# Two-layer DiT trunk with expert mixers: transposed adaptive-norm weights, and the gathered tile's choice of experts moved into the expert loop

## Chip, cores and metric

The kernel runs on one core of one Trainium2 chip. The metric is the device time of one execution in microseconds (us). The engines are named as in the profile: PE (TensorE), PEld (its weight loads), DVE (VectorE), ACT (ScalarE), POOL (GpSimd) and SP (SyncE, which issues most transfers).

## The reference

512 latent tokens of width 1024 go through two layers. Each layer has a mixer (layer 0: latent attention and neighbourhood attention over a shared input projection; layer 1: a conformer convolution) and then an expert mixer with 16,384 experts. Every sub-layer is normalised and modulated by parameters computed from the conditioning vector:

```python
sh1, sc1, g1, sh2, sc2, g2 = ada_params(c, w_ada[l], b_ada[l])     # split(silu(c) @ w + b, 6)
h_lat = h_lat + g1 * mixer(modulate(rms_norm(h_lat, g_norm1[l]), sh1, sc1))
h_lat = h_lat + g2 * peer_ffn(modulate(rms_norm(h_lat, g_norm2[l]), sh2, sc2), ...)

# peer_ffn, per token
q = (hb @ w_query).reshape(128, 8, 2, 128)                 # 8 heads, 2 halves
s = einsum("thpd,hpnd->thpn", q, sub_keys)                 # 16 score rows of 128
s_top, i_top = lax.top_k(s, 16)
best, pos = lax.top_k(s_top[:, :, 0, :, None] + s_top[:, :, 1, None, :], 16)   # of 256 pairs
expert = i_top[0] * 128 + i_top[1] at pos ; gate = softmax(best)
act = gelu(einsum("thkd,td->thk", u_tab[expert], hb))
y = einsum("thk,thkd->td", gate * act, v_tab[expert])
```

`w_ada[l]` is 1024 x 6144. A block below is 128 of its 6144 output features, so there are 48 blocks per layer: 0 to 7 shift 1, 8 to 15 scale 1, 16 to 23 gate 1, 24 to 31 shift 2, 32 to 39 scale 2, 40 to 47 gate 2.

## The kernel before

**Stages.** A preamble loads and normalises and computes blocks 0 to 15 of layer 0 with PE from rows of `w_ada` (L890). The projections follow (`quarter`-wise, each with a weight load, a split into high and low parts `w_hi` and `w_lo`, and three matmuls per product, L145 to L147), then the softmax units of the attention, the out-projection, the expert mixer of layer 0, the convolution, and the expert mixer of layer 1.

**The expert mixer (`peer`).** Of the four tiles of 128 tokens, three (384 tokens) are multiplied densely with all 128 chunks of 128 experts; the fourth, called the gathered tile here, fetches for each token its 128 experts' rows by indirect transfers and works on them with DVE.
- Front: 16 turns `hp`, one for each score row. Turn `hp` issues the load of query weights `wq[hp + 2]` on SP (`load_u`, tile `u_raw`, 3 buffers), 24 matmuls on PE, the split of `wq[hp + 1]` (ACT `u_hi`, POOL `u_lo` L176), the scores of `hp - 1` (L260, copied by ACT L263 to `sc`, 4 buffers), and on DVE `top16` of those scores (two maxima, a replacement and two index searches per tile, for the four tiles in turn) and after each second turn `stage2` (four additions and another `top16`). All queues are in program order and are never reordered.
- Seven dense chunks (EARLY) and beside them `ahead`: gates, ranks and expert numbers (`common`, `numbers`).
- 24 steps of `gbuild`: one-hot tables (L456, 128 x 4096) make the gates of all experts, which go to DRAM (`Gd`) and come back per chunk (`g_in`), while more dense chunks run until 32 are in the ring.
- Expert loop: 96 turns. In each, PE computes the activations of chunk m + 32 (`s1`) and the outputs of chunk m (`s2`, L605); SP loads `u_raw` and `v_raw` (512 KB each); ACT and DVE split them (`u_lo` L176, `v_lo` L584), and DVE makes the weighted activations `w` (L591) and `w_lo` (L596). The gathered tile starts with `decode_last` (9 steps of `lookup`, three a turn), and after it 236 of its 256 row steps lie in the remaining turns. A step is one indirect load on POOL (L616, five `row` buffers) and one DVE product (L624 for the first 128, L628 for the rest).
- Tail: 32 turns with `s2` alone and the last 20 row steps.

**Adaptive-norm blocks (`Ada`).** The other 80 blocks are computed beside other work, each from a load of 512 KB (`ada_w`, 128 x 8 x 128, input features on partitions):
- blocks 16 to 23 of layer 0 in the projections: 8 products on DVE (L766, L768) into `ada_acc`, and a matmul with ones (L907);
- blocks 24 to 39 in the softmax units: products and additions on POOL (L779 to L782), a transpose on PE (L900), and a sum and an addition on DVE (L902, L903);
- 14 blocks of layer 1 in the front of layer 0's mixer (`on_pe`): 8 matmuls each (L819 for columns, L821 for gate rows), 4 more in its `gbuild` steps (`side`), 8 in the front of layer 1's mixer;
- 30 blocks in the expert loop of layer 0 (`slow`): 8 products on DVE over three turns (L866, L868) and one matmul on PE (L883 or L886), which writes into the spare quarter of the `s1` bank.

The gate blocks (`g1`, `g2`) are wanted as rows that stand on all partitions. They go to DRAM as a 128 x 1024 table, block by block, and are loaded from there (`g1b`, `hg`).

## Time and profile before

| | us |
|---|---|
| median of three runs | 3344.88 |
| the profiled execution | 3343.83 |
| its span | 3342.1 |
| PE busy | 3207.8 (96%) |
| DVE busy | 2576.0 (77%) |
| ACT busy | 1288.2 (39%) |
| POOL busy | 976.1 (29%) |
| DMA moved | 764.34 MB, 229 GB/s |

One of the three runs was disturbed (5339.81 us); the other two are 3340.55 and 3344.88. The page divides the span into 40 equal slices and gives the busy share of each engine in tenths; its last lines are the granted clock of PE, the share of the 16 DMA engines and the GB/s:

```profile
PE   8889999988999999999999998988999999999999
```

Each digit is 83.6 us. PE is at nine tenths or more nearly everywhere; the eights are the first 250 us, 668 to 836 us, 2005 to 2089 us and 2172 to 2339 us (the second and the fourth are the one-hot tables of the two layers). Boundaries of the stages, read from the timeline of PE (us from the start of the span): projections 47 to 205, softmax units to 460, out-projection to 504, front of layer 0's mixer to 645, early chunks and ranks to 703, `gbuild` to 875, expert loop to 1671, tail to 1804, convolution to 2062, front of layer 1's mixer to 2187, one-hot tables from 2245, expert loop 2411 to 3204, tail to the end.

### The profile page before, as it was taken

How to read it: one execution, taken by the hardware profiler on the slowest of the kernel's cores; microseconds unless marked ns; L12 is line 12 of the kernel's file. 1: busy time of each engine (PE TensorE's matmuls, PEld its weight loads, DVE VectorE, ACT ScalarE, POOL GpSimd, SP SyncE). 2: the span in 40 equal slices, each digit the busy share in tenths (PEclk: the TensorE clock that was granted, in tenths of full speed). 3: DMA queues.
4: the chain of work that ended last, by engine and by line, in shares of the span. 5: the costliest groups of instructions: out<-in, count | busy, mean ns of one | idle time of the engine just before them, and what ended most of it. 6: DMA issues, size and time to landing. Idle time of an engine off the chain costs nothing.

```text
span 3342.1 us, 45728 instructions
## 1 busy us (share of the span) xinstructions
PE 3207.8 (96%) x16982; PEld 2783.6 (83%) x16982; DVE 2576.0 (77%) x4732; ACT 1288.2 (39%) x2065; POOL 976.1 (29%) x800
## 2 busy tenths in 40 slices
PE   8889999988999999999999998988999999999999
PEld 5775568978999999999987867888999999999987
DVE  3657736889688888888876976899777777777777
ACT  3435533345433333333335234235533333333333
POOL 1347412300033333443430001320033333344330
PEclk9989999999999999999999998999999999999999
DMA  6412124346799999899893113326789888989985
GB/s 199 130 46 79 57 82 152 114 164 252 269 337 328 324 342 333 318 339 336 307 320 119 51 45 112 117 86 247 266 285 314 313 310 315 313 309 314 314 311 180
DMA packets 373679, 764.34 MB, mean 229 GB/s; under 512 B 24144, under 2 KB 221008, under 8 KB 366160
## 3 DMA queue, kind: packets, MB, share of 16 engines
q1 hardware_dynamic: 292816, 442.62, 38.8%
q0 software_dynamic: 73728, 268.47, 22.9%
q10 hardware_dynamic: 6912, 50.33, 3.7%
q8 instruction: 133, 2.18, 0.3%
q14 instruction: 90, 0.74, 0.1%
HBM read 702.61 MB, written 58.72 MB: 228 GB/s over the span
## 4 chain that ended last, share of the span: by engine, by line
PE 83%; DVE 11%; issue 3%; DMA 1%; ACT 1%; SPq 1%; POOL 0%; ACTq 0%; POOLq 0%; DVEq 0%
PE acc L605 30%; PE s L145 11%; PE s L147 11%; PE s L146 11%; DVE eij L456 3%; PE y L1636 2%; PE cz L145 2%; PE cz L147 2%; PE cz L146 2%; DVE ahl L458 1%; PE z L147 1%; PE z L145 1%; PE z L146 1%; PE ot L1421 1%; DVE u_lo L176 1%
## 5 line engine op out<-in xcount | busy, mean ns | idle before, releaser
L146 PE MATMUL s<-hhi,u_lo 128*128 128x384 f32 (+1 forms) x2304 | 791.2, 343 | 14.4 <-DVE u_lo L176 14.2
L145 PE MATMUL s<-hhi,u_hi 128*128 128x384 f32 (+1 forms) x2304 | 798.6, 347 | 3.0 <-ACT u_hi L172 3.0
L147 PE MATMUL s<-hlo,u_hi 128*128 128x384 f32 (+1 forms) x2304 | 790.6, 343 | 0.0
L616 POOL DMA_INDIRECT row<-in_u_dram,eidx x256 | 313.2, 1224 | 954.2 <-DVE row L624 455.7
L616 POOL DMA_INDIRECT row<-in_v_dram,eidx x256 | 348.8, 1362 | 518.8 <-DVE gacc L628 448.4
L582 ACT ACTIVATE v_hi<-v_raw 128x1024 fp32r<-128x1024 f32 x192 | 203.8, 1062 | 679.0 <-PE acc L605 609.9
L146 PEld LDWEIGHTS s<-hhi,u_lo 128*128 128x128 f32 x2304 | 436.2, 189 | 33.2 <-DVE u_lo L176 17.4
L584 DVE TENSOR_TENSOR v_lo<-v_raw,v_hi 128x1024 fp32r<-128x1024 f32 x192 | 235.2, 1225 | 291.4 <-ACT v_hi L582 275.8
L145 PEld LDWEIGHTS s<-hhi,u_hi 128*128 128x128 f32 x2304 | 436.4, 189 | 18.8 <-ACT u_hi L172 3.7
L147 PEld LDWEIGHTS s<-hlo,u_hi 128*128 128x128 f32 x2304 | 435.6, 189 | 10.2
L605 PE MATMUL acc<-v_hi,w_hi 128*128 128x512 f32 x1344 | 417.4, 391 | 0.8 <-ACT w_hi L593 0.8
L605 PE MATMUL acc<-v_hi,w_lo 128*128 128x512 f32 x1344 | 416.2, 391 | 0.0
L605 PE MATMUL acc<-v_lo,w_hi 128*128 128x512 f32 x1344 | 415.9, 390 | 0.0
L176 DVE TENSOR_TENSOR u_lo<-u_raw,u_hi 128x1024 fp32r<-128x1024 f32 x242 | 295.1, 1219 | 48.1 <-ACT u_hi L172 48.0
L628 DVE SCALAR_TENSOR_TENSOR gacc<-row,gwgt,gacc 128x1024 f32<-128x1024 f32 x254 | 325.6, 1282 | 4.7
L172 ACT ACTIVATE u_hi<-u_raw 128x1024 fp32r<-128x1024 f32 x288 | 302.3, 1050 | 14.6 <-ACT stg L475 11.0
L624 DVE SCALAR_TENSOR_TENSOR row<-row,hg 128x1024 f32<-128x1024 f32 x256 | 300.6, 1219 | 0.0
L605 PEld LDWEIGHTS acc<-v_lo,w_hi 128*128 128x128 f32 x1344 | 252.3, 188 | 55.9
L605 PEld LDWEIGHTS acc<-v_hi,w_lo 128*128 128x128 f32 x1344 | 252.2, 188 | 54.6
L605 PEld LDWEIGHTS acc<-v_hi,w_hi 128*128 128x128 f32 x1344 | 249.5, 188 | 40.8 <-ACT w_hi L593 1.2
L593 ACT ACTIVATE w_hi<-w_f 128x384 fp32r<-128x384 f32 x256 | 134.7, 526 | 319.5 <-DVE w_f L591 315.8
L313 ACT ACTIVATE ring<-s 128x384 f32<-128x384 f32 x256 | 125.8, 491 | 318.8 <-PE s L147 318.8
(442 smaller groups left out, 4917.6 us busy)
## 6 DMA issues: line engine op xcount, KB each, us to landing
u_raw<-in_uT_dram SPq DMA_DIRECT2D x256, 512.0 KB
v_raw<-in_v_dram SPq DMA_DIRECT2D x192, 512.0 KB
Gd<-stg ACTq DMA_DIRECT2D x48, 1024.0 KB
g_in<-Gd SPq DMA_DIRECT2D x128, 384.0 KB
ada_w<-in_w_ada_dram SPq DMA_DIRECT2D x80, 512.0 KB
u_raw<-in_v_dram SPq DMA_DIRECT2D x64, 512.0 KB
u_raw<-in_wq_dram SPq DMA_DIRECT2D x32, 512.0 KB
ada_w<-in_w_ada_dram SPq DMA_DIRECT2D x8, 1024.0 KB
```

The lines of the kernel that those rows point to most:

```text
L145: nc.tensor.matmul(out, lhsT=lh, rhs=rh, start=first, stop=False)
L146: nc.tensor.matmul(out, lhsT=ll, rhs=rh, start=False, stop=False)
L147: nc.tensor.matmul(out, lhsT=lh, rhs=rl, start=False, stop=last)
L172: nc.scalar.activation(uh, u, AF.Copy)
L176: lo_eng.tensor_tensor(ul, u, uh.bitcast(F32), op=OP.subtract)
L582: nc.scalar.activation(vh, v, AF.Copy)
L584: nc.vector.tensor_tensor(vl, v, vh.bitcast(F32), op=OP.subtract)
L593: nc.scalar.activation(wh, w, AF.Copy)
L605: nc.tensor.matmul(acc[tt][hf], lhsT=w[:, s], rhs=v[:, hf * 512:(hf + 1) * 512], start=f and n == 0, stop=l and n == 2)
L616: nc.gpsimd.indirect_dma_start(out=r, out_offset=None, in_=un if n < 128 else vn, in_offset=bass.IndirectOffsetOnAxis(ap=eidx[:, c:c + 1], ...
L624: nc.vector.scalar_tensor_tensor(r, r, 1.0, hg, op0=OP.mult, op1=OP.mult, accum_out=act[:, c:c + 1])
L628: nc.vector.scalar_tensor_tensor(gacc, r, wgt[:, c:c + 1], gacc, op0=OP.mult, op1=OP.add)
```

## The change

**Adaptive-norm blocks.** `w_ada` is laid out transposed in DRAM (`wT_ada`, output features on partitions). A block is two halves; each is a load of 256 KB and one DVE `scalar_tensor_tensor` (128 x 512) against `crow`, the row silu(c) that stands on all partitions, with its sum over the free axis accumulated into one column. The tile has two buffers and one load is issued ahead. Neither PE nor POOL takes part, and after each eighth block come two small additions and, for gate blocks, a store to a DRAM row that `gate_row` later reads back on all partitions. `crow` is made in the preamble.

```diff
+    def blocks(self, pool, blocks, pause=0):
+        nc, todo, loaded = self.k.nc, [(f, i) for f in blocks for i in range(2)], []
+        def load():
+            if todo:
+                f, i = todo.pop(0)
+                t = pool.tile([128, D // 2], F32, name="ada_w", bufs=2)
+                nc.sync.dma_start(t, self.wT[f * 128:(f + 1) * 128, i * 512:(i + 1) * 512])
+                loaded.append((f, i, t))
+        load()
+        yield
+        while loaded:
+            load()
+            f, i, t = loaded.pop(0)
+            nc.vector.scalar_tensor_tensor(t, t, 1.0, self.k.crow[:, i * 512:(i + 1) * 512], op0=OP.mult, op1=OP.mult,
+                                           accum_out=self.half[:, f % 8:f % 8 + 1] if i else self.par[:, f:f + 1])
+            if f % 8 == 7 and i:
+                o = slice(f - 7, f + 1)
+                nc.vector.tensor_tensor(self.half, self.half, self.bT[:, o], op=OP.add)
+                nc.vector.tensor_tensor(self.par[:, o], self.par[:, o], self.half, op=OP.add)
+                if f // 8 in self.gate:
+                    nc.sync.dma_start(self.gate[f // 8].rearrange("f p -> p f"), self.par[:, o])
+            for _ in range(1 + pause):
+                yield
...
-    A2 = modulation(k, k.const, g2T[1], ada1.par, 32, "A2_1")      # was behind conv, now ahead of it
```

| where | blocks before | blocks after |
|---|---|---|
| projections | 8 (DVE and PE) | 24, three halves each quarter |
| softmax units | 16 (POOL, PE and DVE) | 20, two halves a call |
| front, layer 0 mixer | 14 (PE) | 16, three halves a turn in turns 0 to 10 |
| `gbuild`, layer 0 mixer | 4 (PE) | none |
| expert loop, layer 0 | 30 (DVE, one matmul) | 12, one half every third turn |
| front, layer 1 mixer | 8 (PE) | none |
| expert loop, layer 1 | none | 8, one half every fourth turn |

**The gathered tile.** In the front, `top16` and `stage2` run over the three dense tiles alone. The fourth tile's scores go to DRAM from ACT's queue, 64 KB a turn. `common` (gates and ranks) also runs over three tiles, and its three copies for the gathered tile fall away. In the expert loop `decode_last` loads the scores back (two loads of 512 KB) and does 16 `top16`, 8 `stage2`, the gates, ranks and lookups on DVE, paced by a table of estimated microseconds. Its gathers begin where the paced sum ends, in turn 15.

```diff
+        nc.scalar.dma_start(Sd[:, hp, :], sc[:, ND, :])
+        pend.append((hp, sc[:, 0:ND]))
...
-            for _ in range(DEC_MAIN):
-                if next(dec, dec) is dec:
+            while m and gfirst is None and spent < DEC_MAIN * m:
+                step = next(dec, None)
+                if step is None:
                     gfirst = m
                     for n in range(PF - LATE):
                         fetch(n)
-                    break
+                else:
+                    spent += step
             goal = 0
         elif m < busy:
-            goal = 236 * (m - gfirst) // (busy - 1 - gfirst)
+            goal = 226 * (m - gfirst) // (busy - 1 - gfirst)
         else:
-            goal = min(256, 236 + (m + 1 - busy))
+            goal = min(256, 226 + -(-30 * (m + 1 - busy) // 25))
```

`DEC_MAIN` is 4.2 now (estimated microseconds a turn), where it was 3 (steps a turn). The weighted activation `w` is computed in place in the ring's tile. All of this is done in both layers.

How the rows of DVE stand in the front of layer 0's mixer: `sc` are the scores of one turn, `S1v` their maxima, `cand` the pair sums, `gp` the PSUM tile of an adaptive-norm block, `crow` the row of silu(c). Before, the first two turns:

```order
L811 TENSOR_TENSOR ada_br<-gp,ada_br 128x128 x2
L222 MAX S1v<-sc 128x8 x4
L224 MATCH_REPLACE s_4295<-S1v,sc 128x128 x4
L226 MAX S1v<-s_4295 128x8 x4
L228 MAX_INDEX I_4061<-S1v,sc 128x8 x4
L230 MAX_INDEX I_4061<-S1v,s_4295 128x8 x4
L811 TENSOR_TENSOR ada_br<-gp,ada_br 128x128
```

After, the same place:

```order
L785 SCALAR_TENSOR_TENSOR ada_w,ada_half_84<-ada_w,crow 128x512
L785 SCALAR_TENSOR_TENSOR ada_w,ada_par_83<-ada_w,crow 128x512
L218 MAX S1v<-sc 128x8 x3
L220 MATCH_REPLACE s_4238<-S1v,sc 128x128 x3
L222 MAX S1v<-s_4238 128x8 x3
L224 MAX_INDEX I_4032<-S1v,sc 128x8 x3
L226 MAX_INDEX I_4032<-S1v,s_4238 128x8 x3
L785 SCALAR_TENSOR_TENSOR ada_w,ada_half_84<-ada_w,crow 128x512
L785 SCALAR_TENSOR_TENSOR ada_w,ada_par_83<-ada_w,crow 128x512
L785 SCALAR_TENSOR_TENSOR ada_w,ada_half_84<-ada_w,crow 128x512
```

Ahead of each turn's maxima DVE now has three products, each of which reads a load, and the maxima are three instead of four.

SP's queue at the same place, where `u_raw` is the load of query weights and `ada_w` that of a block or half block. Before:

```order
L167 DMA u_raw<-in_wq_dram 128x1024
L758 DMA ada_w<-in_w_ada_dram 128x8x128
L167 DMA u_raw<-in_wq_dram 128x1024
L758 DMA ada_w<-in_w_ada_dram 128x8x128
L167 DMA u_raw<-in_wq_dram 128x1024
```

After:

```order
L163 DMA u_raw<-in_wq_dram 128x1024
L778 DMA ada_w<-in_wT_ada_dram 128x512 x3
L163 DMA u_raw<-in_wq_dram 128x1024
L778 DMA ada_w<-in_wT_ada_dram 128x512 x3
L163 DMA u_raw<-in_wq_dram 128x1024
```

One load between two loads of query weights has become three of half the size, and each of them can be issued only when the product before last on DVE has freed its buffer.

PE's queue at the end of the second turn, where `scp` are the scores and `gp` the block. Before:

```order
L145 MATMUL s_4228<-hhi,u_hi 128x512
L146 MATMUL s_4228<-hhi,u_lo 128x512
L147 MATMUL s_4228<-hlo,u_hi 128x512
L821 MATMUL gp<-ada_w,cond 128x128 x16
L260 MATMUL scp<-skt,qt 128x128 x4
L145 MATMUL s_4318<-hhi,u_hi 128x512
```

After:

```order
L142 MATMUL s_4256<-hhi,u_hi 128x512
L143 MATMUL s_4256<-hhi,u_lo 128x512
L144 MATMUL s_4256<-hlo,u_hi 128x512
L256 MATMUL scp<-skt,qt 128x128 x4
L142 MATMUL s_4345<-hhi,u_hi 128x512
```

The matmuls of the blocks are gone from PE (two blocks in this turn, one in the others), and nothing takes their place.

## Rows read from the trace of the kernel before

**Rows 1.** Stretches: length, busy us of PE, PEld, DVE, ACT, POOL, clock, share, GB/s
```profile
504.00:660.00 156.00, 149.86 (x865) 133.18 (x864) 120.71 (x821) 50.23 (x76) 50.85 (x25) 0.98 0.41 135
875.00:1671.00 796.00, 795.24 (x4050) 724.30 (x4049) 682.73 (x1030) 288.81 (x383) 303.73 (x238) 1.00 0.92 327
2410.00:3205.00 795.00, 795.00 (x4020) 723.54 (x4019) 608.17 (x766) 291.80 (x387) 304.72 (x241) 1.00 0.89 308
1675.00:1700.00 25.00, 25.00 (x112) 20.72 (x111) 17.04 (x22) 8.91 (x12) 7.35 (x5) 1.00 1.00 370
```

**Rows 2.** Timeline of PE in the front: start us, us, engine, line, operation
```profile
535.43 0.48 PE L145 MATMUL s<-hhi,u_hi 128*128 128x512 f32 x1
...
540.99 1.95 PE L821 MATMUL gp<-ada_w,cond 128*128 128x128 f32 x16
542.77 1.06 PE L260 MATMUL scp<-skt,qt 128*128 128x128 f32 x8
543.59 0.48 PE L145 MATMUL s<-hhi,u_hi 128*128 128x512 f32 x1
```

**Rows 3.** Timeline of DVE in the front, idle time before it in brackets
```profile
544.50 0.88 DVE L222 MAX8 S1v<-sc 128x8 f32<-128x128 f32 x4 [3.19 <-ACT sc L263]
...
549.19 0.21 DVE L237 TENSOR_TENSOR cand<-S1v 128x64 f32<-128x64 f32 x1
...
553.20 0.27 DVE L811 TENSOR_TENSOR ada_br<-gp,ada_br 128x128 f32<-128x128 f32 x1
```

**Rows 4.** Groups of the whole span: line, shapes xcount, busy us, mean ns, idle before
```profile
L624 DVE SCALAR_TENSOR_TENSOR row<-row,hg 128x1024 f32<-128x1024 f32 x256 | 300.6, 1219 | 0.0
...
L596 DVE TENSOR_TENSOR w_lo<-w_f,w_hi 128x384 fp32r<-128x384 f32 x256 | 141.8, 554 | 44.3 <-ACT w_hi L593 44.3
...
L624 DVE DVE_READ_ACCUMULATOR row<-row,hg 128x1 f32 x256 | 21.1, 82 | 0.0
```

**Rows 5.** Line 768: count, nanoseconds min/median/max, first and last start
```profile
L768 DVE SCALAR_TENSOR_TENSOR ada_acc<-ada_w,cond,ada_acc x56: 350/352/2585, 80.1 to 204.4; 128x128 f32<-128x128 f32 x56
```

**Rows 6.** Chain of waits: a 64 KB and a 512 KB load; start us, us
```profile
164.81 2.23 DMA ada_br<-in_b_ada_dram
...
869.74 4.76 DMA ada_w<-in_w_ada_dram
```

**Rows 7.** Timeline of PE in the projections: where it sat idle
```profile
147.20 0.80 PE L147 MATMUL z<-w_lo,aTl 128*128 128x512 f32 x1 [4.83 <-DVE w_lo L1043]
...
169.21 0.79 PE L147 MATMUL z<-w_lo,aE 128*128 128x512 f32 x1 [5.97 <-DVE w_lo L1043]
...
204.81 0.49 PE L907 MATMUL tp<-ada_acc,ones 128*128 128x128 f32 x2 [3.90 <-DVE ada_acc L768]
```

**Rows 8.** Groups of DVE in the softmax units
```profile
L903 DVE TENSOR_TENSOR ada_par<-ada_par,vec 128x1 f32<-128x1 f32 x16 | 16.5, 1030 | 0.6
```

**Rows 9.** Groups of POOL in the front of layer 0's mixer
```profile
L176 POOL TENSOR_TENSOR u_lo<-u_raw,u_hi 128x1024 fp32r<-128x1024 f32 x21 | 51.1, 2434 | 102.9 <-ACT u_hi L172 102.8
```

**Rows 10.** Timeline of DVE: its wait at the first split behind each front
```profile
675.97 1.23 DVE L176 TENSOR_TENSOR u_lo<-u_raw,u_hi 128x1024 fp32r<-128x1024 f32 x1 [8.38 <-ACT u_hi L172]
...
2218.21 1.23 DVE L176 TENSOR_TENSOR u_lo<-u_raw,u_hi 128x1024 fp32r<-128x1024 f32 x1 [4.55 <-ACT u_hi L172]
```

**Rows 11.** Groups of DVE between that split and the one-hot tables
```profile
L367 DVE COPY d_ab<-stg 128x1024 f16<-128x1024 f16 x2 | 1.3, 686 | 0.0
```

**Rows 12.** Line 456, the one-hot tables: layer 0, then layer 1
```profile
L456 DVE TENSOR_TENSOR eij<-iota,ij x24: 2273/2284/2289, 703.2 to 838.8; 128x4096 f16<-128x4096 f16 x24
...
L456 DVE TENSOR_TENSOR eij<-iota,ij x24: 2283/2284/2295, 2245.5 to 2375.2; 128x4096 f16<-128x4096 f16 x24
```

**Rows 13.** Chain of waits: outputs of three turns of the expert loop
```profile
892.65 4.13 PE acc L605 x18
...
901.18 4.12 PE acc L605 x18
...
909.49 4.12 PE acc L605 x18
```

More of the change, by code (lines that the diff above doesn't have):

```diff
@@ L1 @@
 from contextlib import ExitStack
+from itertools import chain
 import numpy as np
@@ L263, in scores @@
         nc.scalar.activation(sc, p, AF.Copy)
-        pend.append((hp, sc))
+        nc.scalar.dma_start(Sd[:, hp, :], sc[:, ND, :])
+        pend.append((hp, sc[:, 0:ND]))
     ur, us = {}, {}
-    front_step = front and front(qp, lambda: psf.tile([128, TT, 128], F32, name="gp", bufs=4))
+    beside = front(qp) if front is not None else iter(())
     for hp in range(16):
@@ L280, in peer @@
             us[0] = split_u(ur.pop(0), nc.gpsimd)
-        if front_step is not None:
-            front_step()
-            if hp in FRONT_TWICE:
-                front_step()
+        for _ in range(3):
+            next(beside, None)
         qt = qp.tile([128, T], F32, name="qt", bufs=2)
@@ L314, in s1_gelu @@
         ring[c] = r
-    while front_step is not None and front_step():
-        pass
     for c in range(EARLY):
@@ L389, in peer @@
     tr = {}
-    rk = []
+    rk = gp.tile([128, ND, 2, 128, 2], F16, name="d_ab")
     def common():
-        gates_a()
-        yield from ranks(lambda n, shape, dt: gp.tile(list(shape), dt, name=n), TT * 128)
-        gates_b()
+        gates_a(gates, best)
+        room = gp.tile([128, 128, SB], F32, name="stg", bufs=2).rearrange("p a b -> p (a b)").bitcast(F16)
+        yield from ranks(pos.rearrange("p t h k -> p (t h k)"), room, rk)
+        gates_b(gates, gz)
         yield
-        for n, d_ in enumerate((a2l, b2l)):
-            nc.vector.tensor_copy(d_, rk[0][:, ND, n])
-        nc.vector.tensor_copy(i16l, I1[:, ND].rearrange("p (h two) k -> p two h k", two=2))
-        nc.vector.tensor_copy(ggate, gates[:, NTD:T])
     idx = {}
@@ L481, in peer @@
     per_tile = 128 // GB
-    side_step = side and side(gp, lambda: psf.tile([128, TT, 128], F32, name="scp", bufs=2))
     half = {}
@@ L531, in peer @@
             c = dense(c)
-        if side_step is not None:
-            side_step()
-    while side_step is not None and side_step():
-        pass
     while c < RING:
@@ L670, in peer @@
     pdone = 0
-    beside = slow(bs) if slow is not None else None
-    if beside is not None:
-        next(beside)
+    beside = slow(bs)
     dec = decode_last()
+    next(dec)
+    spent = 0.0
     gfirst = None
@@ L711, in peer @@
             gdone += 1
-        if beside is not None and c < NCHUNK:
-            try:
-                beside.send(room)
-            except StopIteration:
-                beside = None
+        next(beside, None)
         if m == busy:
             nc.sync.dma_start(hres, hd)
-            nc.sync.dma_start(hg, g2d)
+            nc.sync.dma_start(hg, gate_row(g2d))
         if m == NCHUNK - 6:
@@ L896, in columns @@
-    def columns(self, p, acc, f, n):
-        nc = self.k.nc
-        for i in range(n):
-            nc.tensor.transpose(p[:, i, :], acc[:, i, :], self.k.ident)
-        o = self.par[:, f:f + n]
-        nc.vector.tensor_reduce(o, p[:, 0:n, :], axis=AX.X, op=OP.add)
-        nc.vector.tensor_tensor(o, o, self.bT[:, f:f + n], op=OP.add)
-    def bcast(self, p, acc, dst, brow):
-        nc = self.k.nc
-        nc.tensor.matmul(p, lhsT=self.k.ones, rhs=acc, start=True, stop=True)
-        nc.vector.tensor_tensor(dst, p, brow, op=OP.add)
+        self.half = k.const.tile([128, 8], F32, name="ada_half%d" % l)
@@ L1117, in attention, with ada_step @@
     r1 = lst.enter_context(k.pool("a_r1"))
-    ada_step = ada.stepper(adp, lambda: psz.tile([128, 4, 128], F32, name="tp", bufs=2), range(16, 16 + B0), HOW[0], k.g1d[0], None)
+    gate_blocks = ada.blocks(adp, range(16, 40))
+    def ada_step():
+        next(gate_blocks, True)
+        next(gate_blocks, True)
+        return next(gate_blocks, True)
     qn = r1.tile([128, 4, 8, 64], F32, name="qn")
@@ L1508, in attention @@
     g1b = hA.tile([128, D], F32, name="g1b")
-    nc.sync.dma_start(g1b, k.g1d[0])
-    ada_ps = lambda: psh.tile([128, 4, 128], F32, name="pt", bufs=3)
-    steps = [ada.stepper(adp, ada_ps, range(16 + B0, 40), HOW[1], None, None)]
+    nc.sync.dma_start(g1b, gate_row(ada.gate[2]))
+    next_blocks = chain(ada.blocks(adp, range(40, 48)), ada1.blocks(adp, range(12)))
     def ada_step():
-        if steps and not steps[0]():
-            steps.pop(0)
-        return steps
+        next(next_blocks, True)
+        return next(next_blocks, True)
     units = [(kind, hd, m) for kind in "nm" for hd in range(8) for m in range(4)]
@@ L1908, in trunk @@
         hs = ExitStack()
[L1909 to L1910 removed]
+        ada0, ada1 = (Ada(k, l, a["wT_ada%d" % l]) for l in range(2))
         R = dict(side="right")
```

288 lines of the change are left out of this document (97 added, 191 removed).

## Prediction

> **What bounds the kernel now.** I read the busy time by stretches first. In the expert loops PE is busy 795.2 of 796 us and 795 of 795, at full clock [rows 1], so there only PE's own instructions count, as long as DVE (682.7 and 608.2 us) and the transfers (share 0.92 at 327 GB/s, 0.89 at 308) keep up. The fronts come next: PE works 149.9 of 156 us, DVE 120.7 [rows 1], and the timeline shows what PE spends on the blocks there [rows 2]. Where PE sits idle I read who ends the wait: in the projections DVE [rows 7], in the one-hot tables DVE itself is the bound. So the change gains where it takes instructions from PE beside a free DVE, or instructions from DVE where DVE is the bound, and it pays where its new products make DVE late.
>
> **The price of a new product.** A half is 128 x 512 with an accumulator. The nearest rows are the 1024-wide product with an accumulator, 1219 ns plus 82 ns to read it, the 384-wide subtraction, 554 ns [rows 4], and the 128-wide product, 352 ns [rows 5]. On the line between 384 and 1024 a 512-wide one takes 0.69 us, 0.77 with the read. Its load of 256 KB lies between 64 KB in 2.23 us and 512 KB in 4.76 [rows 6]: on that line 3.3, in a quiet stretch nearer the lower end; I take 2.8 (2.2 to 4.8). With two buffers the load of half k + 2 is issued when product k has freed its tile, so of three products in one call the first two find their data and the third waits: 0.77 + 2.8 + 0.77, about 4.4 us of DVE a call, of which 2 are waiting.
>
> **Preamble.** `crow` needs one sigmoid on ACT and one 1024-wide product, which stands on DVE ahead of the modulation that the first matmuls wait for: +1.3 us (0 to 2.5).
>
> **Projections.** Three stalls of 4.83, 5.97 and 3.90 us end with DVE behind a block's products [rows 7]: 14.7 us that can go. But every quarter now has a call of 4.4 us, where every second one had the eight products of 0.35 us, and behind the call's third product stand `w_lo` and the evictions. Quarters differ in PE time, so some of these calls will come late again. I expect 12 us of new stalls: −2 (−14 if all hides, +8 if each quarter loses 1.5 us).
>
> **Softmax units.** 16 additions that average 1030 ns for one column [rows 8] (they run beside POOL's products) go, with the transposes and sums, and POOL's work beside the rest. 40 products, 31 us, come in. DVE has room and PE waits for it in places: −5 (−10 to +3).
>
> **Front of layer 0.** A turn of PE is 543.59 − 535.43 = 8.16 us, of which 542.77 − 540.99 = 1.78 are one block [rows 2]. Without it a turn is 6.38, and 14 blocks are 24.9 us. That would be the gain if DVE could follow. DVE's turn: `top16` of four tiles takes 549.19 − 544.50 = 4.69 us, `stage2` 553.20 − 549.19 = 4.01 [rows 3]; for three tiles 3.5 and, with its fixed part, 3.15. With the call of 4.4 and half a `stage2`, a turn is 3.5 + 1.6 + 4.4 = 9.5 us against PE's 6.4, for eleven turns. The queue on SP ties the two: the load of `wq[hp + 2]` stands behind the three half loads of turn hp − 1, which wait for DVE's products. Turn 13 of PE therefore begins no sooner than DVE's call of turn 10 plus that load (4.76) [rows 6], ACT's split, counted as 1, and POOL's (2.43) [rows 9]. DVE is there after 11 x 4.4 + 9 x 3.5 + 4 x 3.15 = 92.5 us, PE then needs 8.2 + 3 x 6.4 more: 120 us, with about 3 us at the start 123, against 16 x 6.38 + 24.9 = 127 before. So of 24.9 us nearly all is taken back: −2 (−25 if DVE's waits don't bind, +12 if each call is 1.3 us longer).
>
> **Ranks.** DVE waited 8.38 us for the chunk at the end of the front and 4.55 in layer 1 [rows 10], so PE's front sets their start and DVE's work from there to the tables is on the path. The 1024-wide copies (686 ns each) shrink by a quarter [rows 11], as do some fifteen smaller ones, and three small copies go: −2.2 in each layer (−1 to −4).
>
> **One-hot tables of layer 0.** From the first to the last table 135.6 us in layer 0, with the four `side` blocks, and 129.7 in layer 1 without them [rows 12]: −5.9.
>
> **Expert loop of layer 0.** A turn with a block's matmul takes 901.18 − 892.65 = 8.53 us, one without 909.49 − 901.18 = 8.31 [rows 13]; 30 of them: −6.
>
> **Front of layer 1.** Eight blocks go and none come: 8 x 1.78 = −14.2, since DVE (2 x 3.5 + 3.15 = 10.2 us in two turns) stays below PE (12.8). With the ranks −16.4. That DVE waited there [rows 10] says that PE's gain is passed on.
>
> **The modulation of layer 1's mixer** moves ahead of the convolution: −1.
>
> **Loops and tails.** The late start of the gathers puts 226 steps in 81 turns, 2.79 a turn instead of 2.54. A turn moves 512 + 512 + 192 KB and 2.79 rows of 512 KB, 2.71 MB in 8.31 us, 326 GB/s, and with the half blocks and stores 334 to 336. Before it was 327 and 308, and a stretch of the tail reached 370 at share 1.00 with PE busy throughout [rows 1]. DVE's turn is 3.55 us of splits and weights, 2.79 x 1.3 and 0.24 for blocks: 7.4 of 8.31; in the first 14 turns the decode is paced to 4.2, 8.0 in all. The tail has 1.2 steps a turn instead of 1. I put +3 for all that (0 to +10).
>
> **Sum.** 1.3 − 2 − 5 − 2 − 2.2 − 5.9 − 6 − 16.4 − 1 + 3 = −36.2 us. From the profiled 3343.83 us (span 3342.1; the median is 3344.88, one us away): about 3308 us.
>
> **A rule beside the rows.** The 128-wide product took 350 to 352 ns in most cases and 2585 in the worst [rows 5], about the length of POOL's split, 2434 ns [rows 9], which POOL does once in each turn of the front; there a product could thus lose up to 2.4 us a turn. The Trainium skill, "SBUF — State Buffer", section "Who interferes with whom", says that a DVE instruction with two SBUF inputs and a GpSimd instruction that reads SBUF exclude each other for their whole length. By that rule, which the worst row agrees with, half of the eleven turns would lose one split, and the front would be 13 us longer than I sum, 3321 us in all.
>
> **Rivals.**
> - *DVE's waits hide.* Loads land in 2.2 us and the queues absorb the rest: the front gains 24.9 instead of 2 and the projections 14 instead of 2, about 3273 us. For it: DVE was idle over 35 of 156 us in the front [rows 1]. Against it: three products need one load after the other in every turn. Chance 0.16.
> - *DVE's calls are dearer.* Products locked out by POOL in the front, and loads over 3.5 us beside query weights: +12 there, +8 in the projections: about 3328. Chance 0.18.
> - *The expert loops become bound by transfers, and the kernel slower.* Both loops now ask for about 335 GB/s over 81 turns of 8.31 us (673 us). If the mix of indirect rows and loads gets no more than some 318 GB/s, each loop loses 5% of 673, 34 us, together 67 against my 3: 3372 us. It decides below about 330 GB/s. For it: share 0.92 already at 327 [rows 1]. Against it: 370 in the tail without a PE stall, and 327 with none in layer 0. Chance 0.08.
> - *The change moves no work off the path* (what PE loses it waits for): within 10 us of before. Chance 0.06.
>
> **Numbers.** My forecast, 3308, holds with 0.52 (own range 3295 to 3322). The range 3270 to 3340 leaves out the loops' bound, half of the case in which nothing comes, and part of the case in which all waits hide. A measurement of this kernel tells about 2%, 67 us, from no change: faster means under 3278 us, which only the first rival reaches, and not always: 0.13. Slower means above 3412: 0.02. Same: 0.85.
>
> **What would show it.** In the front of layer 0: PE stalls that end with `u_lo`, DVE waits that end with a half's load, a turn near 9.5 us, and PE's last score product near 641 to 645 us. In layer 1's front a turn of 6.4 us. In the tables of layer 0 a spacing as in layer 1. In the loops turns of 8.31 us with no stall, at 335 GB/s or less. I am wrong if layer 0's front ends before 630 us, if turns of the loops exceed 8.4 us, or if the projections end later than before.

## The result and the profile after

The changed kernel takes 3377.6 us (median; 3374.31 to 3378.52) where the kernel before takes 3345.36: a ratio of 1.0097 with an interval of 1.008 to 1.0115. The forecast was 3308 us in a range of 3270 to 3340. The kernel became slower by 1%, and the prediction had the sign wrong. The profiled execution took 3374.31 us, its span is 3372.3 us, 30.2 more than before.

The span divides into stages at instructions that both kernels have, read on the timeline: the first matmul of the projections, the first score and the last output matmul of the softmax units, the first and last 512-wide product of each front, the first one-hot table, the first `acc` matmul, the last activation matmul of the loop and the last `acc` matmul. All in us:

| stage | before | after | difference | forecast |
|---|---|---|---|---|
| preamble | 47.4 | 49.3 | +1.9 | +1.3 |
| projections | 187.6 | 187.4 | −0.2 | −2 |
| softmax units | 222.0 | 241.7 | **+19.7** | −5 |
| out-projection and norm | 61.2 | 62.9 | +1.7 | 0 |
| front, layer 0 | 125.1 | 139.5 | **+14.4** | −2 |
| early chunks and ranks, layer 0 | 59.9 | 59.7 | −0.2 | −2.2 |
| tables to first output, layer 0 | 171.6 | 165.8 | −5.8 | −5.9 |
| expert loop, layer 0 | 796.5 | 790.1 | −6.4 | −6 |
| tail, layer 0 | 134.7 | 144.0 | **+9.3** | see below |
| convolution | 264.7 | 262.5 | −2.2 | −1 |
| front, layer 1 | 114.5 | 100.1 | −14.4 | −14.2 |
| early chunks and ranks, layer 1 | 60.2 | 59.7 | −0.5 | −2.2 |
| tables, layer 1 | 165.8 | 165.6 | −0.2 | 0 |
| expert loop, layer 1 | 789.3 | 794.4 | **+5.1** | see below |
| tail, layer 1 | 135.8 | 143.8 | **+8.0** | both loops and tails together +3 |

The three large gains (the tables and the first loop of layer 0, the front of layer 1) came out within half a microsecond. The losses stand in five other places. The rows that answer to the ones of before, first the stretches of the changed kernel (length, busy us of PE, PEld, DVE, ACT, POOL, clock, transfers' share, GB/s), the front of layer 0 and the two loops:

```profile
541.00:681.00 140.00, 114.09 (x499) 92.98 (x500) 106.44 (x558) 33.66 (x50) 39.25 (x16) 0.88 0.37 124
...
875.00:1671.00 796.00, 795.31 (x4063) 726.10 (x4063) 632.14 (x1034) 296.15 (x394) 285.87 (x219) 1.00 0.88 309
...
2410.00:3205.00 795.00, 792.20 (x4008) 722.02 (x4007) 629.23 (x1020) 292.14 (x388) 287.84 (x222) 1.00 0.87 306
...
1040.00:1690.00 650.00, 650.00 (x3288) 591.65 (x3287) 533.28 (x705) 238.40 (x316) 286.21 (x219) 1.00 0.94 335
```

In the front PE is busy 114 of 140 us at a mean clock of 0.88, where [rows 1] had 149.9 of 156 at 0.98. The loops stay full. Their means of 309 and 306 GB/s hold the first turns too, in which no row is gathered; in the turns with gathers (last row) 335 GB/s are moved, as worked out, and PE is busy for all of the 650 us: the rival of transfers did not happen.

**The gate store.** The chain of waits of the changed kernel (start us, us, what) shows what stands at the largest single waits. Softmax units, then the front, then a half load that has no store ahead of it:

```profile
352.02 0.38 SPq L792
352.40 0.05 issue
352.45 12.07 DMA ada_w<-in_wT_ada_dram
```

```profile
612.19 2.58 DMA ada_w<-in_wT_ada_dram
...
622.12 0.38 SPq L792
622.55 12.49 DMA ada_w<-in_wT_ada_dram
```

L792 is the store of a gate's eight columns as rows in DRAM, 1024 elements of 4 bytes. A load of 256 KB issued right behind it on SP lands after 12.1 and 12.5 us; without a store ahead of it, after 2.58. Between 622.5 and 625 us the trace has 1040 packets, all under 512 bytes; for the 8 us behind them hardly anything is moved (12 GB/s, the row's last number):

```profile
624.00:632.00 8.00, 5.95 (x27) 4.77 (x26) 0.00 (x0) 0.00 (x0) 0.00 (x0) 0.91 0.10 12
```

On DVE (idle time in brackets) the load of 622.55 is a wait of 12.43 us, and the ordinary third product of a call waits 2.08:

```profile
614.86 0.70 DVE L785 SCALAR_TENSOR_TENSOR ada_w<-ada_w,crow 128x512 f32<-128x512 f32 x1 [2.08 <-DMA ada_w<-in_wT_ada_dram]
...
635.13 0.69 DVE L785 SCALAR_TENSOR_TENSOR ada_w<-ada_w,crow 128x512 f32<-128x512 f32 x1 [12.43 <-DMA ada_w<-in_wT_ada_dram]
```

PE meets it in its next turns, first for the query weights that SP issued behind those half loads:

```profile
638.11 0.79 PE L142 MATMUL s<-hhi,u_hi 128*128 128x512 f32 x1 [8.16 <-ACT u_hi L168]
640.53 0.79 PE L143 MATMUL s<-hhi,u_lo 128*128 128x512 f32 x1 [1.63 <-POOL u_lo L172]
```

In the second expert loop the store stands ahead of the chunks' own loads on SP; the turn that begins at 2952.6 us is 12.63 us long instead of 8.31. There SP itself is held up. It issues nothing from 2926.84 us until the store goes out at 2940.74, 13.9 us later, right behind DVE's addition that completes the stored columns (at 2940.54); the chunks' loads stand behind it in SP's order:

```profile
2926.41 0.43 SPq L559 DMA_DIRECT2D g_in<-Gd  x1
2940.74 0.38 SPq L792 DMA_DIRECT2D gate<-ada_par  x1
```

**The tails.** DVE's timeline in the tail, one turn with one row step and one with two:

```profile
1727.88 1.28 DVE L611 SCALAR_TENSOR_TENSOR gacc<-row,gwgt,gacc 128x1024 f32<-128x1024 f32 x1
1729.07 1.22 DVE L567 TENSOR_TENSOR v_lo<-u_raw,v_hi 128x1024 fp32r<-128x1024 f32 x1
1730.21 0.55 DVE L574 TENSOR_TENSOR ring<-ring,g_in 128x384 f32<-128x384 f32 x1
1731.43 0.56 DVE L579 TENSOR_TENSOR w_lo<-ring,w_hi 128x384 fp32r<-128x384 f32 x1 [0.67 <-ACT w_hi L576]
1731.91 2.60 DVE L611 SCALAR_TENSOR_TENSOR gacc<-row,gwgt,gacc 128x1024 f32<-128x1024 f32 x2
1734.42 1.22 DVE L567 TENSOR_TENSOR u_lo<-u_raw,u_hi 128x1024 fp32r<-128x1024 f32 x1
1735.56 0.55 DVE L574 TENSOR_TENSOR ring<-ring,g_in 128x384 f32<-128x384 f32 x1
1736.78 0.56 DVE L579 TENSOR_TENSOR w_lo<-ring,w_hi 128x384 fp32r<-128x384 f32 x1 [0.67 <-ACT w_hi L576]
```

The first turn is 4.03 us (1727.88 to 1731.91), the second 5.34 (to 1737.25). PE's turn is 4.15. So one step a turn fits with 0.12 us to spare, and each turn with two, five in a tail, is over by 1.2 us, of which one-step turns give back little. PE then waits for the weights that DVE made late:

```profile
1736.80 0.74 PE L588 MATMUL acc<-u_hi,w_hi 128*128 128x512 f32 x2 [0.89 <-ACT w_hi L576]
```

**The ranks.** DVE waits longer for the chunk ahead of its last ranks, 13.11 us where [rows 10] had 4.55 in layer 1:

```profile
2236.46 1.23 DVE L172 TENSOR_TENSOR u_lo<-u_raw,u_hi 128x1024 fp32r<-128x1024 f32 x1 [13.11 <-ACT u_hi L168]
```

The tables behind it are as forecast; in layer 0 from first to last 129.4 us, as in layer 1 [rows 12]:

```profile
L445 DVE TENSOR_TENSOR eij<-iota,ij x24: 2273/2284/2287, 740.7 to 870.1; 128x4096 f16<-128x4096 f16 x24
```

### The profile page after: what moved, and what is told of

It reads as the page before. It is cut to its first block, busy times and chain, and to the rows that moved or that the text cites. A ratio compares the mean times of both kernels' runs of the same rounds, so it can differ in the third digit from the quotient of the medians.

```text
span 3372.3 us, 44628 instructions
## 1 busy us (share of the span) xinstructions
PE 3185.7 (94%) x16474; PEld 2738.7 (81%) x16474; DVE 2590.8 (77%) x4772; ACT 1296.0 (38%) x2072; POOL 931.1 (28%) x736
## 4 chain that ended last, share of the span: by engine, by line
PE 70%; DVE 16%; DMA 5%; issue 5%; ACT 2%; SPq 1%; POOL 0%; ACTq 0%; DVEq 0%; POOLq 0%
PE acc L588 24%; PE s L143 10%; PE s L144 10%; PE s L142 10%; DVE eij L445 3%; PE y L1531 2%; DMA ada_w<-in_wT_ada_dram 2%; PE cz L142 2%; PE cz L144 2%; PE cz L143 2%; DVE u_lo L172 1%; PE ot L1318 1%; DVE ada_w L785 1%; DVE ahl L447 1%; PE z L144 1%
## 5 line engine op out<-in xcount | busy, mean ns | idle before, releaser
L142 PE MATMUL s<-hhi,u_hi 128*128 128x384 f32 (+1 forms) x2304 | 800.3, 347 | 18.9 <-ACT u_hi L168 18.9
L144 PE MATMUL s<-hlo,u_hi 128*128 128x384 f32 (+1 forms) x2304 | 793.5, 344 | 0.0
L599 POOL DMA_INDIRECT row<-in_u_dram,eidx x256 | 336.0, 1312 | 1049.0 <-PE acc L588 639.4
L576 ACT ACTIVATE w_hi<-ring 128x384 fp32r<-128x384 f32 x256 | 134.6, 526 | 357.0 <-DVE ring L574 341.4
```

The source lines that it names most:

```text
L142: nc.tensor.matmul(out, lhsT=lh, rhs=rh, start=first, stop=False)
L144: nc.tensor.matmul(out, lhsT=lh, rhs=rl, start=False, stop=last)
L576: nc.scalar.activation(wh, w, AF.Copy)
L599: nc.gpsimd.indirect_dma_start(out=r, out_offset=None, in_=un if n < 128 else vn, in_offset=bass.IndirectOffsetOnAxis(ap=eidx[:, c:c + 1], ...
```

## The experiments

The theory: five separate losses, (1) the gate store on SP's queue, (2) DVE's products in the chain of the softmax units, (3) the third product's wait in the front, (4) two row steps in a turn of the tail, (5) DVE's saved work in the ranks is idle time because PE's early chunks stand ahead. The rivals are named with each run. Stage times below are read as in the table above.

**The gate stores on ACT's queue** (one line):

```diff
-                    nc.sync.dma_start(self.gate[f // 8].rearrange("f p -> p f"), self.par[:, o])
+                    nc.scalar.dma_start(self.gate[f // 8].rearrange("f p -> p f"), self.par[:, o])
```

> The four gate stores (a column block stored as a row, 4 bytes an element) are issued from ACT's queue instead of SP's. In the changed kernel the half load that SP issued right behind such a store landed 12.5 us after its issue in the front of layer 0's mixer (DVE waited 12.43 us), another cost DVE 8.44 us in the softmax units, and one turn of the second expert loop took 12.63 us instead of 8.31. Theory A, the store holds up only what stands behind it in its own queue: all three go, softmax units -6 us, front -8 us, second loop -4 us, about -18 us in all (3359 us). Theory B, the store's 1024 small elements occupy the 16 transfer engines for everybody: the waits stay within 2 us, no change (3377 us).

Measured 3349.76 us, 1.0017 of before (1.0006 to 1.0029). Projections 187.4 to 182.1, softmax units 241.7 to 235.9, front 139.5 to 131.8, second loop 794.4 to 790.9: the span falls from 3372.3 to 3350.2. DVE's waits for half loads in the front fall from 32.1 to 22.2 us. The time falls by more than theory A says, since a store in the projections had cost 5 us too. But that the store holds up only its own queue is not what the trace shows. In the front of this run ACT issues the store at 609.88 us. The load of query weights that SP issues 1.02 us later takes 13.62 us, where one without a store ahead of it took 4.84; ACT waits 10.74 us for it, and again hardly anything is moved for 7 us:

```profile
609.88 0.38 ACTq L792 DMA_DIRECT2D gate<-ada_par  x1
610.90 13.62 DMA u_raw<-in_wq_dram
613.00:620.00 7.00, 5.37 (x13) 3.89 (x13) 6.47 (x52) 0.87 (x2) 2.33 (x1) 0.50 0.71 15
```

The same load takes 13.53 and 14.28 us in the two later runs that have this store on ACT's queue and the same front. So theory B is right in this, that a load behind the store is late from another queue too. What the move takes away in the second loop is that SP stands still until DVE has made the columns. In the front it lets the next half load go out 0.41 us ahead of the store (609.47 us) instead of behind it; the product that reads it waits 1.73 us and the one after it 3.74, where the changed kernel had 12.43. No run leaves the store out of the front, so what it still costs there is open. The front's 7.7 us are less sure than the other gains: with the same blocks and the store on ACT's queue the two later runs have 132.0 and 139.2 us there, and the next run below, which leaves the front and the store alone, has 143.0.

**The old tail schedule** (236 row steps in the loop, then one a turn):

```diff
-            goal = 226 * (m - gfirst) // (busy - 1 - gfirst)
+            goal = 236 * (m - gfirst) // (busy - 1 - gfirst)
...
-            goal = min(256, 226 + -(-30 * (m + 1 - busy) // 25))
+            goal = min(256, 236 + (m + 1 - busy))
```

> The gathers' schedule goes back to 236 row steps in the loop and one a turn in the tail (20 turns), where the changed kernel has 226 and then 30 over 25 turns. Theory A, in the tail DVE's turn with two row steps (5.3 us) is longer than PE's 4.15 us and these turns set the loss: the tails shrink from 144.0 to about 135 us each, -16 us in all (3361 us), and the loops stay at 8.31 us a turn although they hold 2.91 steps a turn. Theory B, the loops have no room for 2.91 steps: the loops grow by as much as the tails shrink, no change.

Measured 3362.44 us (1.0054, 1.0028 to 1.008). Tails 144.0 to 135.8 and 143.8 to 136.6, the loops 789.9 and 793.5 as before it: theory A. The loop had the room for ten more steps, the tail had not.

**Three buffers in the front**, two loads ahead:

```diff
-        load()
+        for _ in range(ahead):
+            load()
...
-                t = pool.tile([128, D // 2], F32, name="ada_w", bufs=2)
+                t = pool.tile([128, D // 2], F32, name="ada_w", bufs=1 + ahead)
...
-             open1, done1, beside0, lambda pool: ada1.blocks(pool, range(12, 28)))
+             open1, done1, beside0, lambda pool: ada1.blocks(pool, range(12, 28), 0, 2))
```

> In the front of layer 0's mixer alone the half blocks get three buffers and two loads are issued ahead, so that all three loads of a turn are issued before the turn's first product. Theory A, the third product's wait for its load (2.1 us in most turns) makes DVE the pacer of the front: the front falls from 139.5 us by about 11 x 2.1 = 23 us, less what DVE's other work still holds, to 118 to 125 us (3357 to 3363 us in all). Theory B, the front is paced by the query weights' load that stands behind the half loads on SP, and by the gate store: it falls by less than 6 us.

Measured 3355.12 us (1.0035, 1.0019 to 1.005); the front 118.9 us, 20.6 less, with DVE's waits for half loads at 9.2 us instead of 32.1. Theory A: the front was paced by the third product's wait. The extra buffer also covers most of what the moved store gained (with both edits, below, the front is 117.2).

**No blocks in the softmax units**; their 20 go to the first loop:

```diff
-    next_blocks = chain(ada.blocks(adp, range(40, 48)), ada1.blocks(adp, range(12)))
+    next_blocks = iter(())
...
-            yield from ada1.blocks(pool, range(28, 40), 2)
+            b = chain(ada0.blocks(pool, range(40, 48)), ada1.blocks(pool, [*range(16), *range(32, 40)]))
+            for n, _ in enumerate(b):
+                yield
+                if n % 2:
+                    yield
```

> The softmax units get no blocks; their 20 go to the first expert loop (32 blocks there instead of 12, two halves in three turns), and the front takes blocks 16 to 31 of layer 1 instead of 12 to 27. Theory A, the products on DVE and the gate store are what the softmax units lost (230 us after, 210 before): without them the stage takes 200 to 210 us with PE at full clock, -20 to -30 us (3350 us), and the first loop's turns stay at 8.31 us. Theory B, the units became slow because PE lost the blocks' transposes and with them its full clock: the stage stays above 220 us and the granted clock between 255 and 325 us stays below 0.9. Theory C, transfers bound the loop with 32 blocks in it: its turns grow beyond 8.4 us.

Measured 3353.56 us (1.0023, 1.001 to 1.0037). The stage takes 220.0 us, 21.7 less than in the changed kernel and 2.0 less than before the change; the front, in which the gate store (still on SP) now stands eight products earlier, 131.9. The loop is 6.6 us longer, and all of that is one turn of 14.89 us, which follows a gate store on SP; nearly all others are 8.31. By the difference that is theory A, though not by its 200 to 210 us, which went by a wrong reading of the stage before (210, where the table has 222.0). Theory B falls, since the granted clock between 255 and 325 us is 0.95 without the transposes, and so does theory C.

**What in the softmax units?** Two runs on top of the gate stores' move. In one, PE does four idle transposes with each call:

```diff
             ada_step()
+            f = psh.tile([128, 4, 128], F32, name="pt", bufs=3)
+            for j in range(4):
+                P.transpose(f[:, j, :], k.ident, k.ident)
```

> As the run with the gate stores on ACT's queue, and with each call for blocks in the softmax units PE does four transposes that nobody reads (20 x 4, about 0.9 us a call). In that run the stage took 235.9 us, against 220.0 with no blocks there, with the granted clock at 0.79 to 0.96 between 257 and 355 us. Theory A, the low clock behind PE's gaps is what most of the 16 us are: the extra work fills gaps, the clock in that stretch rises, and the stage takes 231 us or less. Theory B, DVE's two products in the chain of a unit are the loss and the clock only follows: the stage takes 236 us or more.

In the other, a call does one half instead of two, twice as often:

```diff
     def ada_step():
-        next(next_blocks, True)
         return next(next_blocks, True)
...
-        if i % 4 == 0 if kind == "n" else i % 2 == 0:
+        if i % 2 == 0 or kind == "m":
             ada_step()
```

> As the run with the gate stores on ACT's queue, and in the softmax units a call does one half instead of two, twice as often: DVE's work and the transfers are the same, the longest stretch of it in a unit's chain is 0.77 us instead of 1.54. The stage took 235.9 us with two and 220.0 us with none. Theory A, what counts is the length of one stretch (it opens a gap on PE, behind which the clock falls): the stage takes 222 to 230 us. Theory B, what counts is the sum of the work on DVE: 233 us or more.

The stretch from 255 to 325 us (the stage begins at 231 to 239 us) in six kernels: before, after, gate stores moved, that with idle transposes, that with one half a call, and no blocks at all (columns as above; the clock is a mean of the two levels, 1.2 and 2.4 GHz, over the stretch, as a share of the higher):

```profile
255.00:325.00 70.00, 68.09 (x315) 41.70 (x314) 56.09 (x122) 38.47 (x116) 53.00 (x72) 0.95 0.26 79
```

```profile
255.00:325.00 70.00, 61.13 (x240) 35.34 (x241) 42.54 (x104) 29.34 (x90) 22.01 (x41) 0.83 0.20 71
```

```profile
255.00:325.00 70.00, 62.47 (x251) 35.98 (x251) 43.19 (x106) 29.84 (x94) 22.02 (x41) 0.85 0.19 68
```

```profile
255.00:325.00 70.00, 64.64 (x289) 39.13 (x288) 44.89 (x110) 32.00 (x101) 22.01 (x41) 0.91 0.21 71
```

```profile
255.00:325.00 70.00, 65.85 (x300) 39.92 (x300) 51.88 (x128) 37.54 (x114) 19.91 (x40) 0.95 0.22 72
```

```profile
255.00:325.00 70.00, 66.83 (x308) 41.09 (x308) 48.22 (x106) 37.64 (x114) 24.14 (x46) 0.95 0.16 56
```

The stage takes 222.0, 241.7, 235.9, 238.4, 217.0 and 220.0 us in this order; the runs took 3359.55 us with idle transposes (1.0048, 1.0032 to 1.0064) and 3337.77 with one half a call (0.9977, 0.9967 to 0.9988). The idle transposes raise the clock (0.85 to 0.91) and the stage is no shorter; they also take PE's time (15.8 us busy) and slots of the `pt` banks, so that the run doesn't clear the clock of all part. One half a call has the same products, loads and blocks as two, and the stage is 18.9 us shorter, below theory A's 222 to 230, at the clock of the kernel before. The whole stage with two halves a call, then with one:

```profile
231.50:467.40 235.90, 220.82 (x894) 126.03 (x894) 156.82 (x337) 112.96 (x290) 46.54 (x64) 0.91 0.19 65
231.40:448.40 217.00, 208.91 (x894) 121.30 (x894) 149.38 (x337) 113.21 (x290) 45.20 (x64) 0.95 0.22 71
```

The same 894 matmuls keep PE busy for 220.8 and 208.9 us. So 11.9 of the 18.9 us are PE's own work, longer at a lower mean clock (0.91 against 0.95), and 7 are idle time. The sum of DVE's work, theory B, is not the loss: 40 products stand in the stage either way. That it is the length of one stretch alone is argued, not shown, since the run changes two more things. The calls stand at twice as many places, and fewer products meet an instruction of POOL: 11 of 40 are long with two halves a call (7.6 us more than alone) and 6 with one (3.2 us), which is 4.4 of the 7.4 us by which DVE's busy time falls. Where a call of two lies is seen on DVE's timeline of the changed kernel and in PE's wait just behind:

```profile
282.32 0.94 DVE L785 SCALAR_TENSOR_TENSOR ada_w<-ada_w,crow 128x512 f32<-128x512 f32 x1
283.20 0.08 DVE L785 DVE_READ_ACCUMULATOR ada_w<-ada_w,crow 128x1 f32 x1
283.20 0.93 DVE L785 SCALAR_TENSOR_TENSOR ada_w<-ada_w,crow 128x512 f32<-128x512 f32 x1
```

```profile
286.42 0.44 PE L1365 MATMUL pt<-ident,Pr 128*128 128x128 f32 x2 [1.70 <-DVE kT L1266]
```

Two products, 1.74 us (both beside POOL; alone they take 1.54 with their reads), and two copies of `kT` behind them keep the next transposes waiting. The waits of PE for that line are 6.4 us in the run with the stores moved and 2.0 with one half a call.

**The gathered tile's part alone**, on the kernel before (maxima, ranks, scores in DRAM, decode in the loop; blocks and tail schedule as before):

```diff
+        nc.scalar.dma_start(Sd[:, hp, :], sc[:, ND, :])
+        pend.append((hp, sc[:, 0:ND]))
...
+            while m and gfirst is None and spent < DEC_MAIN * m:
```

> The kernel before with the gathered tile's part of the change alone: its choice of experts in the expert loops, the front's maxima and the ranks over three tiles, the adaptive-norm blocks as before, and the old tail schedule (236 row steps in the loop, 20 in the tail). Theory A (the prediction's), DVE's ranks are on the path: -2.2 us a layer and more, 3338 to 3341 us. Theory B, DVE waited there for PE's early chunks and in the front for PE's scores, so what it no longer does was idle time: 3343 to 3348 us; any gain of this part comes only with the blocks gone from PE. Theory C, the decode in the loop costs: 3350 us or more, in the first 15 turns of each loop.

Measured 3350.06 us (1.0022, 1.0012 to 1.0031). Fronts 125.1 and 114.4 and ranks 59.5 and 59.7 us against 125.1, 114.5, 59.9 and 60.2: nothing gained, and the first loop 4.1 us longer, in one turn of 13.41 us at its start. DVE's wait ahead of its last ranks is 13.11 us in layer 0 now, where [rows 10] had 8.38:

```profile
677.13 1.23 DVE L175 TENSOR_TENSOR u_lo<-u_raw,u_hi 128x1024 fp32r<-128x1024 f32 x1 [13.11 <-ACT u_hi L171]
```

For the fronts and ranks that is theory B. The time is theory C's (6 us slower, 0.12 to 0.31%), and most of it stands where C puts it, at the first loop's start; what makes that turn long was not tried.

**The four together**, then **48 blocks in the first loop** and none in the front, then that with **four early chunks** (`EARLY, LEFT = 4, 5`):

> The four changes together: gate stores from ACT's queue, the old tail schedule, three buffers in the front, the softmax units' blocks in the first expert loop. Theory A, the four losses are separate: stage by stage the shortest of the single runs add up (projections 182, softmax 220, front about 112, tails 136 each, the rest as in the changed kernel), 3296 to 3304 us. Theory B, they share causes (transfers, or DVE in the loop that now has 32 blocks and 2.91 row steps a turn): the first loop grows by 10 us or more and the time stays above 3315 us.

> As the four together, but the front of layer 0 has no blocks at all (so two buffers do) and the first expert loop has 48, one half every turn. DVE then needs 3.55 + 2.91 x 1.3 + 0.77 = 8.1 us of a turn of 8.31 and the transfers ask for about 360 GB/s. Theory A, the loop still hides them: the front takes 16 x 6.38 = 102 us, -8 against the four together, 3288 to 3296 us. Theory B, the loop is full: its turns pass 8.4 us, and what the front gains comes back, 3300 us or more.

> As the one with 48 blocks in the loop, and four dense chunks instead of seven stand ahead of the ranks (the other three go beside the one-hot tables). In the changed kernel DVE waited 13.1 us there in layer 1 for PE's chunk. Theory A, the ranks are held up by these chunks, not by their own length: three chunks of 4.17 us move behind DVE's work, which gets three splits of 1.22 us more, -8 to -9 us a layer, 3272 to 3280 us. Theory B, PE has no room beside the tables: no gain.

Measured 3307.39 us (0.9897, 0.988 to 0.9913), 3295.96 (0.9861, 0.9844 to 0.9877) and 3280.37 (0.9814, 0.9798 to 0.9831). The first is a little over its range (projections 183.0, front 117.2, tails 136.6 and 136.4): the losses are separate but for the front, where three buffers and the moved store take away the same wait. The second: front 100.0, loop 794.8, with one turn of 12.15 us and two near 9, so theory A with a tax of 4 us. The third: 12.6 and 12.5 us less in the ranks, 5 more from the tables to the first output, −7.3 and −7.4 a layer. Four early chunks on the kernel before were not tried, so how much of this comes without the shorter ranks is open. DVE's wait there is 0.98 us in layer 1:

```profile
2195.96 1.23 DVE L172 TENSOR_TENSOR u_lo<-u_raw,u_hi 128x1024 fp32r<-128x1024 f32 x1 [0.98 <-ACT u_hi L168]
```

**Blocks out of the decode's turns**, and **everything that the single runs recommend**. The first:

```diff
+            b = chain(ada0.blocks(pool, range(40, 48)), ada1.blocks(pool, range(40)))
+            next(b)
+            yield
+            for m in range(1, 128):
+                if 13 < m < 96 or m > 112:
+                    next(b, None)
+                yield
```

> As the run with 48 blocks in the first loop and four early chunks (3280.4 us), but the blocks leave out the 13 turns in which the gathered tile's choice of experts is made, and go on behind the last row step of the tail. In that run the first loop took 792.7 us with two turns of 10.2 and 8.9, and its tail 139.2 us. Theory A, blocks and decode together overfill DVE there: the loop takes 790.3 us and the tail 136 to 137 us, -4 us (3276 us). Theory B, these turns are long for another reason: no change.

> What the single runs recommend, in one kernel: gate stores from ACT's queue, the old tail schedule, one half block a call in the softmax units (20 blocks, as in the changed kernel), none in the front, 28 blocks in the first loop from its 14th turn on, one half a turn, and four early chunks. Theory A, the gains are separate: softmax units 217 to 219 us, front 100, first loop 790, tails 136 each, 3272 to 3280 us, and below the run with 48 blocks in the loop (3280 us) by some 3 us. Theory B, the softmax units' gain was luck of that run (it began at a higher clock): 3280 us or more.

Measured 3282.78 us (0.9818, 0.9802 to 0.9835) and 3274.93 (0.9798, 0.9782 to 0.9814). In the first the loop falls from 792.7 to 790.3 us and the tail from 139.2 to 137.3, as in theory A, but the time does not fall (3282.78 against 3280.37, the same within the intervals): in the profiled execution the projections (184.1) and the convolution (265.5) took 4.7 us more than in the run that it changes. The last is the best, and it repeats the gain of one half a call: softmax units 217.7, fronts 100.0 and 100.2, first loop 791.7, tails 136.4 and 136.4. In a stretch of its first loop 336 GB/s are moved, and PE never waits there:

```profile
1500.00:1600.00 100.00, 100.00 (x507) 91.02 (x506) 83.79 (x85) 36.68 (x49) 45.00 (x35) 1.00 0.95 336
```

## Why the prediction was wrong, step by step

The sum said −36.2 us and the span grew by 30.2, 66 us apart. By the table, 24.7 of them lie in the softmax units, 19.4 in the second loop and the tails, 16.4 in the front of layer 0, 3.7 in the ranks and 2.2 in the rest. Across these stages four steps failed: the gate stores had no term, DVE's idle time in the softmax units was taken for room, the tail's turns were not summed, and the ranks were put on the path. Two of the named signs of being wrong came, and neither through its own stage: the projections ended 1.8 us later, by the preamble, and one turn of the second loop passed 8.4 us, by the store.

- **Preamble, tables, first loop, layer 1's front, the earlier modulation**: right, within a microsecond each (the convolution gained 2.2 for 1). A turn of PE in layer 1 is 6.35 us, forecast as 6.38:

```profile
2152.29 1.05 PE L256 MATMUL scp<-skt,qt 128*128 128x128 f32 x8
...
2158.64 1.05 PE L256 MATMUL scp<-skt,qt 128*128 128x128 f32 x8
```

- **Price of a product**: 0.69 us and 0.08 for the read, as interpolated; a load of 256 KB 2.6 us for 2.8, the third product's wait 2.1 for 2.
- **The gate store was not in the sum.** The text says "with the half blocks and stores" for the transfers' demand and prices no store. With the stores on ACT's queue four stages are 3.5 to 7.7 us shorter each, 22 together (the medians are 27.8 apart). This is the step that most of all failed: an issue was counted by its bytes (4 KB), not by its 1024 elements, nor by what SP had queued behind it while the columns were not yet made. The Trainium skill, "DMA: Bandwidth & Descriptors", section "Rules for kernel authors", says that a transfer whose last dimension is strided becomes one descriptor per element. The trace agrees, with 1040 packets under 512 bytes behind the issue; no run here has the same store with longer pieces, so that the 10 us are the price of its pieces is not shown.
- **Softmax units (−5, measured +19.7).** "DVE has room and PE waits for it in places" took the mean share of DVE for room. About 6 us are the gate store; the rest, 16 us against the stage without blocks, comes with two products in one call, since two calls of one cost nothing. What was wrong is that 1.54 us of DVE were compared with idle time summed over the stage, not with the slack of the chain of one unit at the place of the call. The lower clock (0.83) goes with the gaps, and 11.9 us of the loss are PE's own work taking longer beside 7 of waiting; that the clock is a cause by itself was not shown.
- **Front of layer 0 (−2, measured +14.4).** The mechanism was as forecast: DVE's call paces the front through SP's queue, and with a third buffer 20.6 us go. The price of a call was about right for an undisturbed one (4.0 us from 611.57 to 615.56, forecast 4.4). The sum was too small by the gate store, with one wait of 12.43 us in place of 2.08, and by products beside POOL's split: six of the 32 took 8.0 us more than they do alone, where the prediction weighed 13 and left it out of its sum. One such pair, DVE and then POOL:

```profile
581.51 2.82 DVE L785 SCALAR_TENSOR_TENSOR ada_w<-ada_w,crow 128x512 f32<-128x512 f32 x1
```

```profile
581.09 2.69 POOL L172 TENSOR_TENSOR u_lo<-u_raw,u_hi 128x1024 fp32r<-128x1024 f32 x1 [10.28 <-ACT u_hi L168]
```

  The product ends just behind POOL's split (584.33 and 583.78 us), 2.1 us later than alone; that was the rule weighed in the prediction (the Trainium skill, "SBUF — State Buffer", "Who interferes with whom"), and the trace agrees with it. Of the rivals, the dearer calls came in the front, in part by the store, and not in the projections. The front with blocks and two buffers came out at 131.8 to 143.0 us in runs whose edits don't touch its products; why it varies stays open.
- **Ranks (−2.2 a layer, measured −0.2 and −0.5).** That DVE waited was read as "DVE's work from there to the tables is on the path". But most of the work that shrinks stands in DVE's order ahead of that wait, and what it saved made the wait longer (4.55 to 13.11). Only what stands behind it counts.
- **Tails (within the +3 for loops and tails, measured +9.3 and +8.0).** I named 1.2 steps a turn and did not compare DVE's turn with PE's 4.15 us. The rows of DVE in the tail would have given it: a turn with one step takes 4.03 us, start to start, with a wait of 0.67 for ACT in it, and a second step adds 1.3. Moving steps from the tail back to the loop took 8.2 and 7.2 us off the tails. In layer 1's loop the +5.1 are mostly the store's (4.3 us in one turn).
- **The rivals.** The loops did not become bound by transfers: 335 GB/s in the turns with gathers of the changed kernel's first loop and 336 in a stretch of the best one's, with PE busy throughout. That part of the sum was right. The time landed on the slower side by mechanisms that stood in no rival.

## What to carry to other kernels

Count a transfer by its elements as well as by its bytes, and look at what stands behind it. A small store with 4-byte pieces belongs on a queue where no load waits for the data that it stores, and at a time when no load is wanted soon: the other queue did not free the loads behind it. Work that is put "beside" a stage is to be compared with the slack at the very place where it goes, turn by turn, and cut as fine as the calls allow: two half-size calls were free where one full one cost 16 us (whether by its length or by its place was not separated). Where an engine waits, work saved ahead of the wait is worth nothing until the wait itself is moved: with four early chunks instead of seven, 7 us a layer came.

## What the runs showed of the hardware that was not expected

A store of 1024 elements of 4 bytes held up the transfers issued just behind it, whichever queue it went out on. From SP's queue, a load of 256 KB on SP took 12.5 us to land instead of 2.58; from ACT's queue, a load of 512 KB on SP took 13.62 us instead of 4.84. For 7 to 8 us behind the small packets only 12 to 15 GB/s were moved. A product that met POOL's split took 2.82 us instead of 0.69.
